# The second output gate of a sequence-encoder trunk, with 512- and 256-column products, a split moved to GpSimd, and two small moves

## The chip, the cores and the metric

The kernel runs on one NeuronCore of a Trainium2 chip. The metric is the device time of one execution in microseconds; three executions of the kernel before were timed, and one more was profiled. TensorE (PE in the rows) does the matrix products and the loads of their stationary operands, VectorE (DVE), ScalarE (ACT) and GpSimd (POOL) do the elementwise work, SyncE (SP) and ScalarE issue the DMAs used here.

## The reference, cut to what matters

Two layers work on x of 256 positions by 1024 channels, in float32. Each layer mixes tokens (an mLSTM branch beside a convolution branch), attends to 256 memory tokens and applies a gated FFN. The part touched here:

```python
h = rmsnorm(x, norm_mix[l])
p = h @ w_in[l] + b_in[l]
y_m = mlstm_branch(p[..., :o1], p[..., o1:o2], ...)
y_c = conformer_conv_branch(p[..., o2:o3], p[..., o3:o4], ...)   # conv of 31 taps -> layernorm -> silu -> @ w_pw
merged = sigmoid(p[..., o4:o5]) * y_m + sigmoid(p[..., o5:]) * y_c
x = x + merged @ w_out[l]
```

The first gate, sigmoid(p[o4:o5]), is called g1 below, the second g2.

## The kernel before, in words

**Numbers as two parts.** Every large product is computed from float32 numbers that are split into a high part (rounded to the engine's fast format) and the rest, the low part. A product is the sum of three: high by high, high by low and low by high. Activations stand channel by position: 8 channel tiles of 128 rows, each with 256 high and 256 low columns side by side. Weights come in chunks of 256 output columns, a chunk as two halves of 128; one half and its 8 channel tiles are one block of PE's work.

**Two forms of a block.** `three` (L100 to L104) runs, for each channel tile, three products of 256 columns into one accumulator of 256 columns: 24 products, each with a weight load of its own. `two` (L90 to L98) runs 8 products of 512 columns, high weights by high and low activations at once, into an accumulator of 512 columns, and then 8 products of 256 columns, low weights by high activations, into its second part: 16 products, 16 loads and as many columns in sum. The two parts of that accumulator must then be added: `joined` (L281) copies the second part to a scratch tile on ACT (L285, or L287 with a bias) and adds it to the first on DVE (L288). `proj` (L299) takes `two` with halves=True. In mix(), mdown uses `two` for chunks 0 and 1 and pw for chunks 0 to 2; g1 and g2 use `three`.

**Weights.** `weights` (L194) runs loads and splits ahead of use: a load of 1 MB a chunk by DMA (L169), then for each half the high part on ACT (L184, a cast of 1024 columns) and the low part either on DVE (L190, one subtraction of 1024 columns) or, where the table ON_POOL (L39) names the chunk, on POOL (L188, two of 512 columns). Splits run four halves ahead of the products. Five split halves and three raw chunks fit at a time.

**Accumulators.** Blocks go to three PSUM banks in turn (`acc`). A bank is free when the last reader of its block is done; for pw that is the split of the merged result (ACT L267, DVE L268).

**Order.** Each engine runs its instructions in a fixed order. The framework lays that order down when the kernel is built, from the program's order, priorities and its own model of the durations. The list `portions` holds small pieces of work (convolution taps on DVE, then the layer norm) of which a few are taken after each block (`taps`).

**Start.** The first chunk is used unsplit, in full float32 (`proj_first`, L291). emit_loads (L159) issues its first half in two pieces and its second half whole on SP's queue (L166), while ACT's queue brings x in four pieces (L211); then ACT loads its function table and computes one dummy value (L225). Chunks 1 and 2 are loaded from ACT's queue (L169) as soon as x is being scaled (L979, L273). Here x is scaled by the norm's weights alone; the row of 1/rms is multiplied into the results later. The sums of squares for it are products with a column of means (`stats`, L333), followed by an addition on DVE (L336) and a power on POOL (L338); `to_row` (L372) spreads the result over rows with four small products (L324) and a copy on ACT (L377). Where these stand among PE's products is given by hooks, (half, channel tile) of a chunk: (0, 7) and (1, 6) everywhere.

**Layer norm of the convolution.** POOL adds the four pairs of channel tiles into ysum (L495), two tiles wide, the last pair when the last tap is done. `ln_mean` (L696) multiplies both tiles of ysum by a matrix of 1/1024 on PE in full float32 (L699). Then come the differences (L703), squares (L706) and their sums.

Of the kernel before, what the change touches and what calls it, by code (L numbers as in the profile page):

```python
# [11 lines left out]
ALU = mybir.AluOpType  # L12
# [7 lines left out]
KT = D // P  # L20
# [16 lines left out]
HEADS_AT = ((0, 1), (2, 3), (), ())  # L37

ON_POOL = {"xm": (3,), "g": (0, 1, 2, 3), "a": (0, 1, 2, 3), "k": (0, 1, 2, 3), "v": (0, 1),  # L39
           "z": (0, 2, 3), "pw": (1, 3), "g1": (0, 1, 2, 3), "g2": (0, 1), "wo": (0, 1, 2),  # L40
           "uv": tuple(range(1, 11))}


# [14 lines left out]
def trunk(ctx, tc, xT, memT, pvec, wgr, w_in, ml_w_down, cv_w_pw, w_out, xa_wq, xa_wk, xa_wv, xa_wo,  # L58
# [100 lines left out]
    def emit_loads(upto):  # L159
        while st["dma"] < min(upto, len(chunks)):  # L160
            i = st["dma"]
            ap = chunks[i][1]
            raws[i] = wraw.tile([P] + list(ap.shape[1:]), F32, tag="raw", name=nm("raw"))
            if i == 0:
                for j, sl in ((0, slice(0, KT // 2)), (0, slice(KT // 2, KT)), (1, slice(0, KT))):
                    nc.sync.dma_start(raws[i][:, j, sl], ap[:, j, sl])  # L166
                halves.extend(raws[0][:, j] for j in range(2))
            else:
                (nc.scalar if i <= LATE_LOADS else nc.sync).dma_start(raws[i], ap)  # L169
            st["dma"] += 1  # L170
# [46 lines left out]
    with tc.high_priority():  # L217

        nc.vector.memset(mean1, 1.0 / D)
        early = sm([P, P])  # L220
        for _ in range(WARM):
            nc.tensor.matmul(early, mean1, mean1, start=True, stop=True)
        nc.vector.memset(zero1, 0.0)
        with tc.issue_after(loaded.ins):
            table = nc.scalar.activation(const.tile([4, 1], F32, name="early"), zero1, AF.Silu)  # L225
    make_identity(nc, ident)
    mhalf = const.tile([P, 8], F32, name="mhalf")
    nc.gpsimd.memset(mhalf, -0.5)
# [28 lines left out]
    def col(l, name, i, n=1):  # L257
        o = _COLS[name] + i
        return pvs[l][:, o:o + n]
# [39 lines left out]
    def proj(key, x2, hooks=None, halves=False, bank=None):  # L299


        done = []
        for j, w in weights(key):
            ps = (bank or acc)([P, 2, S] if halves else [P, S])
            if halves:
                last["pe"] = two(ps, [(w[:, :, k, :], x2[:, k]) for k in range(KT)], True, True)
                yield j, ps
                continue
            for k in range(KT):
                last["pe"] = three(ps, w[:, :, k, :], x2[:, k], k == 0, k == KT - 1)  # L310
                if hooks and (j, k) in hooks:
                    with tc.issue_after(last["pe"].ins):
                        hooks[j, k]()
            if hooks:
                done.append((j, ps))
            else:
                yield j, ps
        yield from done
# [97 lines left out]
    def mix(l, x):  # L416
        xc, hs = planes("xch")
        at, ready, norms = int(l == 0), [], list(range(4))
        hooks = x.hooks()
        for i in range(4):  # L420
            for j, ps in (proj_first(("xm", l, i), xf) if l + i == 0 else
                          proj(("xm", l, i), x.u, hooks if i == at else None, bank=sm if i == 1 and at else None)):
# [59 lines left out]
        def glu(i):  # L482
            sg = t2(F32, "sg")
            for j, ps in proj(("g", l, i), x2):
                last["act"] = nc.scalar.activation(sg[:, j, :], ps, AF.Sigmoid,
                                                   bias=col(l, "b_in", 24 + 2 * i + j))
                taps(TAPS["glu"])
            for j, ps in proj(("a", l, i), x2):
                c = 2 * i + j
                nc.vector.scalar_tensor_tensor(u31[:, c, CK - 1:], ps, col(l, "b_in", 16 + c), sg[:, j, :],  # L490
                                               op0=ALU.add, op1=ALU.mult)
                taps(TAPS["glu"])
            portions.append(lambda: conv31(i))
            if i > 0:
                portions.append(lambda: nc.gpsimd.tensor_tensor(  # L495
                    ysum, u31[:, 0:2, CK - 1:] if i == 1 else ysum, u31[:, 2 * i:2 * i + 2, CK - 1:], op=ALU.add))

        ysum = t2(F32, "ysum")
        glu(0)
# [195 lines left out]

        def ln_mean():  # L696
            ln["pm"] = sm([P, S])
            for n in range(2):
                nc.tensor.matmul(ln["pm"], mean1, ysum[:, n, :], start=(n == 0), stop=(n == 1))  # L699

        def ln_square(c2):
            sl = slice(2 * c2, 2 * c2 + 2)
# [12 lines left out]

        for n, o, dst in (("g1", 32, s1), ("g2", 40, s2)):
            for i in range(4):
                for j, ps in proj((n, l, i), x2):
                    c = 2 * i + j
                    nc.scalar.activation(dst[:, c, :], ps, AF.Sigmoid, bias=col(l, "b_in", o + c))  # L720
                    taps(TAPS["g"])
        while portions:
# [251 lines left out]

    x = Stream(0, "nmix")
    xf = planes("xf")[0]
    with tc.high_priority(), tc.issue_after(table.ins):
        for c in range(8):
            nc.vector.tensor_scalar(xf[:, c, :], xs[:, c, :], col(0, "nmix", c), None, op0=ALU.mult)  # L979
            x.split(c)  # L980
            if c == 3:
                emit_loads(2)
        emit_loads(3)
        nc.scalar.dma_start(pvs[0][:, KT:], pvec[0][:, KT:])
# [98 lines left out]
```

## Time and profile before

| | |
|---|---|
| median of 3 timed executions | 1071.78 us (1070.57 to 1072.33) |
| the profiled execution, its own time | 1070.13 us |
| its span, first to last instruction | 1068.4 us |
| mean granted TensorE clock | 0.998 of full speed |
| PE busy | 1057.0 us (99%), 7166 products |
| DVE, ACT, POOL busy | 853.4 us (80%), 699.2 us (65%), 438.5 us (41%) |
| share of the chain that ended last | PE 48% by the page's list, all of its lines products |

A PE product's duration in the trace contains its way through the pipeline, so products overlap: 256 columns show 0.28 us, but start 0.12 us apart. What a stage costs is read from the starts.

### The profile page before, as it was taken

The page shows a single profiled execution, that of the slowest core. Times are in us where ns is not written, and L with a number is a line of the kernel's source. Part 1 is how long each engine was busy: PE and PEld are TensorE (multiplying, and loading weights), DVE is VectorE, ACT ScalarE, POOL GpSimd, SP SyncE. Part 2 cuts the span into 40 slices and gives each one's busy share as a digit, 9 for nine tenths or more (in the row PEclk, how much of TensorE's full clock was granted, in tenths as well). Part 3 has the DMA queues.
Part 4 walks back from the last instruction along what each step waited for, and adds up shares of the span by engine and source line. Part 5 has one row for each costly group of instructions (what it writes and reads, how often), then busy time and mean ns, then how long its engine had stood idle before and what let it go on. Part 6 is the DMA issues. An engine that isn't in the chain of part 4 may idle for free. (4 is left out here: it accounts for less than half of the span.)

```text
span 1068.4 us, 18718 instructions
## 1 busy us (share of the span) xinstructions
PE 1057.0 (99%) x7166; PEld 977.8 (92%) x7166; DVE 853.4 (80%) x1731; ACT 699.2 (65%) x1152; POOL 438.5 (41%) x351
## 2 busy tenths in 40 slices
PE   8999999999999999999999999999999999999997
PEld 8999889999998988888899998999999989888886
DVE  5899898988857887786587988998788589787753
ACT  5887576466655787774477766565655658877642
POOL 2869568414041354520056784781210414535000
PEclk9999999999999999999999999999999999999999
DMA  8545436455533465555555364555465345555551
GB/s 288 186 149 163 153 122 234 159 198 197 191 129 121 153 203 200 190 197 182 191 179 190 120 198 140 197 170 194 148 222 174 119 158 173 183 197 178 178 197 39
DMA packets 46777, 185.84 MB, mean 174 GB/s; under 512 B 3168, under 2 KB 3168, under 8 KB 44128
## 3 DMA queue, kind: packets, MB, share of 16 engines
q1 hardware_dynamic: 44128, 176.70, 48.5%
q10 hardware_dynamic: 2560, 7.96, 2.2%
q8 instruction: 56, 0.92, 0.3%
q14 instruction: 33, 0.27, 0.1%
HBM read 183.60 MB, written 1.05 MB: 173 GB/s over the span
## 5 line engine op out<-in xcount | busy, mean ns | idle before, releaser
L188 POOL TENSOR_TENSOR wsp<-raw,wsp 128x512 fp32r<-128x512 f32 x312 | 406.0, 1330 | 274.6 <-ACT wsp L184 261.1
L184 ACT CAST wsp<-raw 128x1024 fp32r<-128x1024 f32 (+2 forms) x342 | 352.4, 1036 | 148.8 <-PE acc L104 60.3
L190 DVE TENSOR_TENSOR wsp<-raw,wsp 128x1024 fp32r<-128x1024 f32 (+2 forms) x186 | 233.6, 1258 | 65.5 <-ACT wsp L184 63.0
L477 DVE SCALAR_TENSOR_TENSOR cv<-u,pv,cv 128x256 f32<-128x256 f32 x464 | 193.6, 479 | 2.8 <-ACT cv L470 2.7
L102 PE MATMUL acc<-x,wsp 128*128 128x256 f32 x640 | 182.7, 286 | 0.0
L103 PE MATMUL acc<-x,wsp 128*128 128x256 f32 x640 | 182.0, 284 | 0.0
L104 PE MATMUL acc<-x,wsp 128*128 128x256 f32 x640 | 181.4, 284 | 0.0
L95 PE MATMUL acc<-x,wsp 128*128 128x512 f32 x576 | 144.2, 392 | 0.0
L103 PEld LDWEIGHTS acc<-x,wsp 128*128 128x128 f32 x640 | 122.7, 192 | 0.4 <-issue 0.2
L102 PEld LDWEIGHTS acc<-x,wsp 128*128 128x128 f32 x640 | 122.6, 192 | 0.4 <-issue 0.2
L104 PEld LDWEIGHTS acc<-x,wsp 128*128 128x128 f32 x640 | 122.7, 192 | 0.0
L95 PEld LDWEIGHTS acc<-x,wsp 128*128 128x128 f32 x576 | 103.6, 189 | 18.5
L338 POOL TENSOR_TENSOR rv<-rv,mhalf 128x2 f32<-128x2 f32 x8 | 6.5, 816 | 231.4 <-DVE rv L336 231.4
L878 DVE SCALAR_TENSOR_TENSOR fy<-u,pv,fy 128x256 f32<-128x256 f32 x176 | 84.1, 484 | 20.4 <-ACT fy L875 19.1
L102 PE MATMUL acc<-u,wsp 128*128 128x256 f32 x352 | 99.7, 286 | 0.0
L103 PE MATMUL acc<-u,wsp 128*128 128x256 f32 x352 | 99.7, 284 | 0.0
L104 PE MATMUL acc<-u,wsp 128*128 128x256 f32 x352 | 99.4, 283 | 0.0
L97 PEld LDWEIGHTS acc<-x,wsp 128*128 128x128 f32 x576 | 78.6, 190 | 5.6
L97 PE MATMUL acc<-x,wsp 128*128 128x256 f32 x576 | 80.3, 282 | 0.0
L103 PEld LDWEIGHTS acc<-u,wsp 128*128 128x128 f32 x352 | 67.5, 192 | 0.3
L104 PEld LDWEIGHTS acc<-u,wsp 128*128 128x128 f32 x352 | 67.4, 192 | 0.0
L102 PEld LDWEIGHTS acc<-u,wsp 128*128 128x128 f32 x352 | 67.1, 192 | 0.2
(302 smaller groups left out, 2143.2 us busy)
## 6 DMA issues: line engine op xcount, KB each, us to landing
raw<-in_w_in_dram SPq DMA_DIRECT2D x45, 1024.0 KB, 4.9
raw<-in_ffn_w_up_dram SPq DMA_DIRECT2D x44, 1024.0 KB, 4.8
raw<-in_w_down_last_dram SPq DMA_DIRECT2D x10, 1024.0 KB, 4.8
raw<-in_xa_wk_dram SPq DMA_DIRECT2D x8, 1024.0 KB, 4.8
raw<-in_xa_wv_dram SPq DMA_DIRECT2D x8, 1024.0 KB, 5.1
raw<-in_ml_w_down_dram SPq DMA_DIRECT2D x8, 1024.0 KB, 4.8
raw<-in_cv_w_pw_dram SPq DMA_DIRECT2D x8, 1024.0 KB, 4.9
raw<-in_w_out_dram SPq DMA_DIRECT2D x8, 1024.0 KB, 5.0
```

What stands on the lines that cost most here:

```text
L95: nc.tensor.matmul(ps, a[:, 0], b, start=first and n == 0, stop=False)
L97: mm = nc.tensor.matmul(ps[:, 1], a[:, 1], b[:, 0], start=False, stop=last and n == len(pairs) - 1)
L102: nc.tensor.matmul(ps, a[:, 0], b[:, 0], start=first, stop=False)
L103: nc.tensor.matmul(ps, a[:, 0], b[:, 1], start=False, stop=False)
L104: return nc.tensor.matmul(ps, a[:, 1], b[:, 0], start=False, stop=last)
L184: nc.scalar.copy(hi, r)
L188: nc.gpsimd.tensor_tensor(lo[:, sl], r[:, sl], hi[:, sl].bitcast(F32), op=ALU.subtract)
L190: nc.vector.tensor_tensor(lo, r, hi.bitcast(F32), op=ALU.subtract)
L338: nc.gpsimd.tensor_tensor(rv, v, mhalf[:, 0:2], op=ALU.pow)
L477: nc.vector.scalar_tensor_tensor(o, u31[:, c, k:k + S], col(l, "cdw", c * CK + k), cv[j], op0=ALU.mult, op1=ALU.add)
L878: nc.vector.scalar_tensor_tensor(y[:, j, :], u[:, j, k:k + S], col(l, "fdw", 3 * c + k), y[:, j, :], op0=ALU.mult, op1=ALU.add)
```

## The change

g2 takes `two` for all four chunks, with `joined` (at a priority raised by 100) ahead of its sigmoid; chunk 2 of g2 and chunk 2 of pw get their low parts on POOL; the second half of the first chunk is loaded from ACT's queue, behind x and behind ACT's dummy value, and the scaling of x is put behind that load; the hooks of mix() stand at (1, 1) and (1, 6) in layer 0 (chunk 1) and at (0, 7) and (1, 7) in layer 1 (chunk 0); POOL adds the two tiles of ysum into one, and ln_mean multiplies that one alone.

```diff
-           "z": (0, 2, 3), "pw": (1, 3), "g1": (0, 1, 2, 3), "g2": (0, 1), "wo": (0, 1, 2),
+           "z": (0, 2, 3), "pw": (1, 2, 3), "g1": (0, 1, 2, 3), "g2": (0, 1, 2), "wo": (0, 1, 2),
...
-                for j, sl in ((0, slice(0, KT // 2)), (0, slice(KT // 2, KT)), (1, slice(0, KT))):
-                    nc.sync.dma_start(raws[i][:, j, sl], ap[:, j, sl])
+                for sl in (slice(0, KT // 2), slice(KT // 2, KT)):
+                    nc.sync.dma_start(raws[i][:, 0, sl], ap[:, 0, sl])
...
             table = nc.scalar.activation(const.tile([4, 1], F32, name="early"), zero1, AF.Silu)
+
+        with tc.issue_after(table.ins):
+            loaded = nc.scalar.dma_start(raws[0][:, 1], chunks[0][1][:, 1])
...
-        hooks = x.hooks()
+        hooks = {(1, 1): x.stats, (1, 6): x.to_row} if at else {(0, 7): x.stats, (1, 7): x.to_row}
...
+            if i == 3:
+                portions.append(lambda: nc.gpsimd.tensor_tensor(ysum[:, 0], ysum[:, 0], ysum[:, 1], op=ALU.add))
...
-            for n in range(2):
-                nc.tensor.matmul(ln["pm"], mean1, ysum[:, n, :], start=(n == 0), stop=(n == 1))
+            nc.tensor.matmul(ln["pm"], mean1, ysum[:, 0, :], start=True, stop=True)
...
-                for j, ps in proj((n, l, i), x2):
+                for j, ps in proj((n, l, i), x2, halves=n == "g2"):
                     c = 2 * i + j
+                    if n == "g2":
+                        with tc.high_priority(offset=100):
+                            ps = joined(ps)
                     nc.scalar.activation(dst[:, c, :], ps, AF.Sigmoid, bias=col(l, "b_in", o + c))
                     taps(TAPS["g"])
...
-    with tc.high_priority(), tc.issue_after(table.ins):
+    with tc.high_priority(), tc.issue_after(loaded.ins):
         for c in range(8):
             nc.vector.tensor_scalar(xf[:, c, :], xs[:, c, :], col(0, "nmix", c), None, op0=ALU.mult)
```

## Rows read from the trace of the kernel before

**Rows 1.** The page, busy time by engine: us, share of the span, instructions.
```profile
PE 1057.0 (99%) x7166; PEld 977.8 (92%) x7166; DVE 853.4 (80%) x1731; ACT 699.2 (65%) x1152; POOL 438.5 (41%) x351
```
**Rows 2.** Timeline, layer 0, end of g2 and start of mdown: start, us, engine, line.
```profile
191.46 0.47 ACT L720 ACTIVATE xch<-acc,pv 128x256 f32<-128x256 f32 x1 [1.47 <-PE acc L104]
...
214.50 0.48 ACT L720 ACTIVATE xch<-acc,pv 128x256 f32<-128x256 f32 x1 [1.47 <-PE acc L104]
...
220.91 2.00 PE L95 MATMUL acc<-o,wsp 128*128 128x512 f32 x8
...
223.70 0.63 PE L95 MATMUL acc<-o,wsp 128*128 128x512 f32 x2
```
**Rows 3.** The stretch 197 to 221 us, busy us of each engine, PEclk, DMA share, GB/s.
```profile
197.00:221.00 24.00, 24.00 (x199) 23.89 (x198) 20.45 (x41) 12.65 (x19) 4.56 (x3) 1.00 0.40 140
```
**Rows 4.** The scratch tile of joined: minimum, median, maximum ns, first and last start.
```profile
L288 DVE TENSOR_TENSOR acc<-acc,wh x20: 417/433/433, 226.3 to 786.7; 128x256 f32<-128x256 f32 x20
L285 ACT COPY wh<-acc x8: 372/373/373, 223.9 to 757.4; 128x256 f32<-128x256 f32 x8
```
**Rows 5.** Timeline of PE around ln_mean, layer 0.
```profile
216.69 0.28 PE L104 MATMUL acc<-x,wsp 128*128 128x256 f32 x1
216.81 1.02 PE L699 MATMUL sm<-ysum,mean 128*128 128x256 f32 x4
...
217.79 0.28 PE L103 MATMUL acc<-x,wsp 128*128 128x256 f32 x1
```
**Rows 6.** POOL's additions into ysum: one line's instructions, then the last of layer 0.
```profile
L495 POOL TENSOR_TENSOR ysum<-u x2: 1288/1292/1297, 142.5 to 661.9; 128x512 f32<-128x512 f32 x2
...
212.57 3.18 POOL L495 TENSOR_TENSOR ysum<-ysum,u 128x512 f32<-128x512 f32 x1 [14.19 <-DVE u L477]
```
**Rows 7.** Timeline of PE, layer 1, the row of 1/rms.
```profile
542.60 0.28 PE L104 MATMUL acc<-u,wsp 128*128 128x256 f32 x1
543.09 0.71 PE L324 MATMUL sm<-ident,rv 128*128 128x128 f32 x4 [0.21 <-POOL rv L338]
```
**Rows 8.** Timeline of the start, all engines.
```profile
7.11 0.61 DVE L979 TENSOR_SCALAR xf<-xs,pv 128x256 f32<-128x256 f32 x2 [6.05 <-DMA xs<-in_xT_dram]
...
9.08 1.93 DVE L979 TENSOR_SCALAR xf<-xs,pv 128x256 f32<-128x256 f32 x6 [1.35 <-DMA xs<-in_xT_dram]
9.09 0.39 ACTq L169 DMA_DIRECT2D raw<-in_w_in_dram  x1
...
9.49 6.31 PE L296 MATMUL acc<-xf,raw 128*128 128x256 f32 x28 [0.84 <-DVE xf L979]
...
13.91 2.00 ACT L184 CAST wsp<-raw 128x1024 fp32r<-128x1024 f32 x2 [2.02 <-DMA raw<-in_w_in_dram]
```
**Rows 9.** Stretches of the start; the last two numbers are DMA share and GB/s.
```profile
8.00:9.00 1.00, 0.65 (x4) 0.22 (x2) 0.00 (x0) 0.00 (x0) 0.00 (x0) 1.00 0.92 356
9.00:10.00 1.00, 0.51 (x2) 0.49 (x3) 0.92 (x4) 0.92 (x3) 0.00 (x0) 1.00 0.15 57
10.00:11.00 1.00, 1.00 (x6) 0.87 (x6) 0.92 (x5) 1.00 (x3) 0.00 (x0) 1.00 0.96 139
```
**Rows 10.** Timeline of PE, layer 0, statistics and row.
```profile
19.60 1.05 PE L333 MATMUL cm<-mean,sq 128*128 128x1 f32 x8 [0.43 <-DVE sq L990]
...
22.86 0.60 PE L324 MATMUL sm<-ident,rv 128*128 128x128 f32 x4
```
**Rows 11.** Timeline of the stage pw, layer 0: PE, DVE, POOL.
```profile
264.59 0.39 PE L102 MATMUL acc<-c,wsp 128*128 128x256 f32 x1 [0.28 <-DVE g L268]
...
245.94 1.98 DVE L190 TENSOR_TENSOR wsp<-raw,wsp 128x1024 fp32r<-128x1024 f32 x1
...
257.45 1.23 DVE L190 TENSOR_TENSOR wsp<-raw,wsp 128x1024 fp32r<-128x1024 f32 x1
...
262.97 1.23 DVE L190 TENSOR_TENSOR wsp<-raw,wsp 128x1024 fp32r<-128x1024 f32 x1
...
252.06 5.13 POOL L188 TENSOR_TENSOR wsp<-raw,wsp 128x512 fp32r<-128x512 f32 x4 [0.73 <-ACT wsp L184]
```

## The prediction, made before the changed kernel was run

> **What bounds the kernel now.** I read the page's busy times first: PE is busy 99% of the span, DVE 80%, ACT 65%, POOL 41% [rows 1]. Because products overlap in the trace I then read PE's timeline by starts. From the first block at full pace to the last, PE's products follow each other almost everywhere at their own distance; what a change takes out of PE's queue comes off the time, and what it does to the other engines counts only where one of them makes PE wait. So I looked for the places where PE waits: the start, where it waits for x and then for the sum of squares [rows 8, 10]; the row of 1/rms in layer 1 [rows 7]; and one accumulator in the stage pw [rows 11]. The change touches all three, and PE's own work in two more.
>
> **Part 1, g2 as two products.** A block of `three` takes 2.88 us: the sigmoids behind nine such blocks start at 191.46 to 214.50, eight distances in 23.04 us [rows 2]. A block of `two` takes 2.79 us, from 220.91 to 223.70 [rows 2]: as many columns, eight weight loads fewer. That is 0.087 us a block by the finer starts, call it 0.09; 8 blocks in each of 2 layers give 16 x 0.09 = 1.4 us. A rule of the Trainium skill (TensorE: Matmul & The Clock Gate, section Back-to-back issue gap) puts a product at its columns divided by 2.4 GHz plus 2.5 ns, which would leave only 2.5 ns for each pair made into one, an estimate of 16 x 8 x 2.5 ns = 0.3 us, and 2.4 us instead of 3.5 for the whole sum. I take the rows, since both forms stand in them at the full clock.
>
> What it adds lies on the other engines: per block a copy on ACT of 0.37 us and an addition on DVE of 0.43 us [rows 4]. In the stretch of g2 ACT has 24 - 12.7 us free and DVE 24 - 20.5 us [rows 3]; 8 x 0.43 = 3.5 us would fill DVE, but the two low parts of chunk 2 (2 x 1.23 us, [rows 11]) leave it. Who waits behind these? The bank of a block is held through copy, addition and sigmoid. With a cast of 1.0 us [rows 8] in front of each ACT step and a subtraction of 1.2 us in front of DVE's, that is 1.0 + 0.4 + 1.2 + 0.4 + 1.0 + 0.5 = 4.5 us, and PE comes back to the bank after two blocks, 5.6 us. I cost it at nothing; if that cover were gone, it would be up to 1 us in a layer.
>
> **Part 2, ln_mean.** Its four records (two products, each in two passes) put 217.79 - 216.69 = 1.10 us between products that would stand 0.24 apart without them: 0.86 us, 0.43 for one product [rows 5]. One goes, in two layers: 0.86 us. In its place POOL adds 256 columns. POOL's own rows show 1.29 us for 512 [rows 6], so 0.65 us, up to half of 3.18 = 1.6 where it is held up as the last one was [rows 6]. ysum is complete at 212.57 + 3.18 = 215.75, and PE takes it up at 216.81: 1.06 us to spare [rows 5, 6]. After the change PE arrives 0.6 us sooner (six and a half g2 blocks) and ysum 0.65 to 1.6 later, so if PE's order keeps its place it may wait 0.2 to 1.2 us in a layer. The order is laid down anew, though, with the addition in it, so I take no wait and keep 1.1 us a layer for the bounds; nor do I take a gain there.
>
> **Part 3, the row in layer 1.** PE stands from 542.72 (0.12 after 542.60) to 543.09 for the power on POOL [rows 7]. Three products more, 0.36 us, go in front of the row: -0.36 us, and the row comes when it came before.
>
> **Part 4, the first loads.** x lands late: DVE scales two tiles at 7.11, then waits, and the rest starts at 9.08; PE starts its steady run at 9.49 [rows 8]. The second half of chunk 0, 0.5 MB, travels among x on the other queue. At 356 GB/s [rows 9] it takes 1.4 us; put behind x it lets x finish about 1.3 us sooner, and PE's run starts near 8.2. That is not yet the gain, for what follows hangs on chunk 1: its DMA is issued at 9.09, when x is there, and its cast waits until 13.91 [rows 8]. The queue is nearly empty from 9 to 10 and slow until 11 (57 and 139 GB/s, [rows 9]). Now the half chunk fills that hole: x done near 7.8, chunk 1 issued then, the half chunk done near 10.3, and chunk 1's 1 MB at some 380 GB/s behind it near 13.0, 0.9 us sooner than now. Casts, squares and their sums follow in order on ACT and DVE, and PE's place for the row is bound by that chain (19.60 to 22.86 is statistics, addition, power and nothing else [rows 10]), so 0.9 us it is. Bounds: +0.5 us, if the half chunk is late for PE's second block (needed near 10.4, there near 10.3), and -2.0 us, if both PE's waits at the start and the one at 19.60 go.
>
> **Part 5, the hooks of layer 0.** The statistics move six products later: PE waited at least 0.43 us at that place [rows 10]. But the row stays at (1, 6), and between the two are then 15 products, 1.8 us, for a chain of 3.26 us less the statistics' own 0.9. What is saved at the first place is waited for at the second: 0.
>
> **Part 6, pw's chunk 2 on POOL.** At 264.59 PE has waited for a bank, 0.28 us by the row [rows 11] and 0.44 by the starts, and layer 1 does the same. The bank is freed by DVE's split, which stands behind a subtraction of 1.23 us at 262.97 [rows 11]; that one belongs to the next weight (out) and stays. DVE loses the subtraction at 245.94 [rows 11] and the one after it, but it had idle time between its steps again before the next, at 257.45 [rows 11]. So I take 0. Bounds: -0.9 us (both waits go, by a new order) and +1.5 us: POOL, now with twelve instructions instead of eight, works until about 259 rather than 252.06 + 5.13 = 257.19 and meets the subtraction at 257.45 [rows 11]. What such a meeting costs is shown at 245.94, where the subtraction took 1.98 instead of 1.23 us beside POOL: 0.75 us, in two layers.
>
> **The sum.** -1.4 - 0.86 - 0.36 - 0.9 + 0 + 0 = -3.5 us. The profiled execution took 1070.13 us with its span of 1068.4; it becomes 1066.6. That execution lies 1.65 us under the median of the three shown, so against the median I say 1071.78 - 3.5 = 1068.3 us.
>
> **Rivals.** (a) *The pw wait goes too, or the start gives more.* A new order puts DVE's split ahead of the subtraction: 0.9 us more, 1067.4; with a start at its bound, 1066.3. For it: DVE has 2.5 us less to do there; against: the wait stands at an instruction that stays. (b) *The gains of PE are waited away:* PE meets ln_mean before POOL's second addition in both layers, -3.5 + 2 x 1.1 = -1.3, or the start gives nothing besides; 1070.5 to 1071.4. For it: the last addition took 3.18 us instead of 1.29 [rows 6]; against: the order has room for POOL's step. (c) *POOL holds DVE, slower:* each subtraction on DVE that meets one of POOL's waits for its end, up to 1.3 us. If POOL's four added instructions push its work so far that the three subtractions from 257.45 to 262.97 all meet one, DVE's chain is 3.9 us late in each layer, PE waits that at the banks, and 7.8 - 3.5 = +4.3 gives 1076.1. It decides from 5.6 us of such waits in all on. For it: the two durations above; against: PE's blocks let POOL finish by about 259, and only one subtraction lies before that. The Trainium skill (SBUF — State Buffer, section Who interferes with whom) says that a DVE instruction with two SBUF inputs and a GpSimd instruction that reads SBUF exclude each other for a whole instruction, whichever began first; 1.98 against 1.23 us and 3.18 against 1.29 agree with that. (d) *Fewer loads give nothing but the issue,* as the rule under part 1 has it: -2.4, 1069.4. The rows speak against it at every block of either form. (e) *The change does not do what it says at the start:* x is slow for another reason than the half chunk, -2.6, 1069.2; at 8 to 9 us the queues run at 356 GB/s, which speaks for shared bandwidth.
>
> **The numbers.** A measurement of this kernel can tell about 0.2%, 2.1 us, from no change. Forecast 0.42, (a) 0.18, (d) 0.02, (e) 0.10: all faster by more than that, 0.72. (b) 0.23: within it. (c) 0.05: slower. The range leaves out (c) and the far ends of (a) and (b): 1066.0 to 1070.9. It takes in the bounds of parts 4 and 6.
>
> **What would show it.** In the changed profile: g2 blocks of 2.79 us and 128 fewer products in g2; two records instead of four at ln_mean and no wait in front of them; no wait in front of layer 1's row; x scaled without a break from about 7.7 and chunk 1 cast near 13.0; the wait of 0.44 us at pw unchanged. The forecast is wrong if PE waits for POOL at ln_mean, if a wait in pw grows past 1 us, if a bank is waited for in g2 or mdown, or if chunk 1 is cast no sooner than before.

## The result, and the profile after

The changed kernel is slower: 1082.16 us (median of 4 runs, 1081.69 to 1083.14) against 1071.82 us before (1070.57 to 1072.33), a ratio of 1.0104 with a 95% interval of 1.0091 to 1.0116. The forecast was 1068.3 us, faster. The profiled execution took 1083.14 us, its span is 1081.4 us against 1068.4. In the changed file the lines stand three to seven further down: the norm's products L699 are L703, the row L324 is L327, the power L338 is L341, the additions of `joined` L288 are L291 and its copies L285 are L288, the taps L477 are L480, ysum's additions L495 are L498, and L501 is the new one.

First the page's busy times of the changed kernel, beside [rows 1].

```profile
PE 1060.1 (98%) x7034; PEld 974.4 (90%) x7034; DVE 849.9 (79%) x1739; ACT 704.6 (65%) x1168; POOL 458.0 (42%) x369
```

132 products are gone, as planned (128 in g2, 4 at ln_mean), and yet PE is busy longer. Stretches at a lower clock are what lengthens products; they will be seen below. The list of PE's waits of the changed kernel (engine, line, what it waited for: us in total, times, longest) names the places where it stands still (the three longest in total of eight lines; the others lie at the start or are 0.5 us or less):

```profile
PE sm L703 <- POOL ysum L501: 4.8, 2, 2.6
PE sm L327 <- POOL rv L341: 4.4, 1, 4.4
PE acc L102 <- DVE g L271: 1.5, 2, 1.2
```

**The start.** Timeline of the changed kernel, DVE, ACT, POOL and PE between 6 and 28 us (answers to [rows 8, 10]):

```profile
6.55 2.46 DVE L986 TENSOR_SCALAR xf<-xs,pv 128x256 f32<-128x256 f32 x8 [5.49 <-DMA xs<-in_xT_dram]
...
12.84 1.99 ACT L184 CAST wsp<-raw 128x1024 fp32r<-128x1024 f32 x2 [2.69 <-DMA raw<-in_w_in_dram]
...
20.66 0.15 DVE L339 TENSOR_SCALAR rv<-cm 128x2 f32<-128x2 f32 x1
...
21.55 1.99 ACT L184 CAST wsp<-raw 128x1024 fp32r<-128x1024 f32 x2 [2.74 <-DMA raw<-in_w_in_dram]
...
22.68 2.48 POOL L188 TENSOR_TENSOR wsp<-raw,wsp 128x512 fp32r<-128x512 f32 x2 [19.88 <-ACT wsp L184]
25.12 0.71 POOL L341 TENSOR_TENSOR rv<-rv,mhalf 128x2 f32<-128x2 f32 x1
...
21.19 0.28 PE L104 MATMUL sm<-u,wsp 128*128 128x256 f32 x1
25.89 1.22 PE L327 MATMUL sm<-ident,rv 128*128 128x128 f32 x4 [4.42 <-POOL rv L341]
```

x is scaled without a break from 6.55, and chunk 1 is cast at 12.84 instead of 13.91: the early part is about 1.1 us ahead. At 20.81 the sum of squares is ready for POOL's power. But in POOL's order the power now stands behind two splits of the last chunk of xm, and these wait for a cast at 21.55, which waits for its DMA. The power begins at 25.12, and PE, whose last product before the row starts at 21.19, stands for it until 25.89: 4.57 us by the starts, that is the distance between two starts less the usual one (0.12 us after 256 columns, 0.23 after 512). DVE's step (L339) comes late too: the statistics' products end at 18.52 + 1.05 = 19.57, but two subtractions stand in front of it until 20.66. In the kernel before, the order was the other way round:

```profile
20.94 1.62 POOL L338 TENSOR_TENSOR rv<-rv,mhalf 128x2 f32<-128x2 f32 x1 [18.14 <-DVE rv L336]
22.89 5.07 POOL L188 TENSOR_TENSOR wsp<-raw,wsp 128x512 fp32r<-128x512 f32 x4 [0.34 <-ACT wsp L184]
```

And the wait has an echo. Stretches of the changed kernel, busy us of PE, PEld, DVE, ACT, POOL, then PEclk, DMA share, GB/s:

```profile
24.00:25.00 1.00, 0.00 (x0) 0.00 (x0) 0.00 (x0) 0.00 (x0) 1.00 (x1) 0.72 0.95 389
25.00:27.00 2.00, 1.11 (x5) 1.11 (x6) 0.00 (x0) 0.00 (x0) 2.00 (x3) 0.50 0.12 43
27.00:31.00 4.00, 4.00 (x21) 4.00 (x21) 2.69 (x7) 3.60 (x8) 3.40 (x4) 0.50 0.40 108
```

While PE stands, the granted clock falls to 0.50, the level of 1.2 GHz, and stays there for some 5.4 us after PE has resumed. Products of 256 columns then start 0.21 us apart instead of 0.12:

```profile
28.83 0.41 PE L102 MATMUL acc<-u,wsp 128*128 128x256 f32 x1
29.04 0.41 PE L103 MATMUL acc<-u,wsp 128*128 128x256 f32 x1
```

About 2.5 of these 5.4 us are lost, by comparison with the same products in the first experiment below, which run at full clock. At PE's first products with the memory tokens the changed kernel is 5.48 us behind the kernel before, 88.59 against 83.11:

```profile
88.59 0.50 PE L336 MATMUL sm<-mean,mem 128*128 128x1 f32 x4
```

**The norm of the convolution.** PE, DVE and POOL around ln_mean of the changed kernel, layer 0 (answers to [rows 2, 5, 6]):

```profile
218.92 2.00 PE L95 MATMUL acc<-x,wsp 128*128 128x512 f32 x8
...
221.71 1.09 PE L95 MATMUL acc<-x,wsp 128*128 128x512 f32 x4
225.07 0.70 PE L703 MATMUL sm<-ysum,mean 128*128 128x256 f32 x2 [2.26 <-POOL ysum L501]
...
205.56 0.43 DVE L291 TENSOR_TENSOR acc<-acc,wh 128x256 f32<-128x256 f32 x1 [1.97 <-ACT wh L288]
205.90 2.05 DVE L480 SCALAR_TENSOR_TENSOR cv<-u,pv,cv 128x256 f32<-128x256 f32 x5
208.35 0.43 DVE L291 TENSOR_TENSOR acc<-acc,wh 128x256 f32<-128x256 f32 x1 [0.40 <-ACT wh L288]
...
220.31 0.87 DVE L480 SCALAR_TENSOR_TENSOR u<-u,pv,cv 128x256 f32<-128x256 f32 x2
...
221.26 2.10 POOL L498 TENSOR_TENSOR ysum<-ysum,u 128x512 f32<-128x512 f32 x1 [12.15 <-DVE u L480]
223.43 1.58 POOL L501 TENSOR_TENSOR ysum<-ysum 128x256 f32<-128x256 f32 x1
```

A block takes 221.71 - 218.92 = 2.79 us, as forecast. But DVE has lost its lead. POOL takes up the last pair, with the last tap done, at 221.26; PE would have come to ln_mean at 225.07 - 2.43 = 222.64, only 1.4 us later. In the kernel before it was 212.57 for 216.81 [rows 5, 6], 4.2 us, and DVE then had nothing to do but to wait for the mean:

```profile
217.88 0.69 DVE L703 TENSOR_TENSOR u<-u,sm 128x512 f32<-128x512 f32 x1 [3.18 <-PE sm L699]
```

In the changed kernel, at 205.56, DVE stands 1.97 us in front of the first addition of `joined`, which needs PE's block and ACT's copy, and then 0.4 us in front of three of the following. POOL needs 2.10 + 1.58 us, and PE stands 2.43 us by the starts (2.73 in layer 1). In this execution a stretch at half clock follows both waits; it begins as PE resumes or shortly after, not while PE stands (at 225.07 PE resumes, and from 225 to 226 the mean is still 0.91):

```profile
225.00:226.00 1.00, 0.93 (x4) 0.83 (x5) 0.19 (x1) 0.00 (x0) 0.01 (x1) 0.91 1.00 414
226.00:229.00 3.00, 3.00 (x13) 2.71 (x12) 1.69 (x3) 0.63 (x1) 0.00 (x0) 0.50 0.19 76
...
748.00:751.00 3.00, 2.99 (x7) 2.42 (x8) 1.75 (x3) 1.25 (x3) 0.00 (x0) 0.51 0.54 220
```

**pw.** Layer 0 of the changed kernel, PE's wait for a bank, DVE and POOL in front of it (answers to [rows 11]):

```profile
274.38 0.39 PE L102 MATMUL acc<-c,wsp 128*128 128x256 f32 x1 [1.21 <-DVE g L271]
...
265.91 2.87 DVE L190 TENSOR_TENSOR wsp<-raw,wsp 128x1024 fp32r<-128x1024 f32 x1
...
257.61 10.08 POOL L188 TENSOR_TENSOR wsp<-raw,wsp 128x512 fp32r<-128x512 f32 x8
```

DVE's subtraction meets the last of POOL's splits, which follow each other without a break, and takes 2.87 us instead of 1.23. The 1.64 us more are longer than one of these splits (10.08 / 8 = 1.26 us): it was held past one and through the next. PE's wait grows from 0.44 to 1.37 us by the starts. In layer 1 it stays at 0.44.

**The row of layer 1** comes without a wait, and across it the changed kernel gains the forecast 0.36 us:

```profile
552.75 0.28 PE L104 MATMUL acc<-u,wsp 128*128 128x256 f32 x1
552.88 0.49 PE L327 MATMUL sm<-ident,rv 128*128 128x128 f32 x2
```

### The profile page after: what moved, and what is told of

Read it like the earlier page. It is cut to its first block, busy times and chain, and to the rows that moved or that the text cites. A ratio compares the mean times of both kernels' runs of the same rounds, so it can differ in the third digit from the quotient of the medians.

```text
span 1081.4 us, 18513 instructions
## 1 busy us (share of the span) xinstructions
PE 1060.1 (98%) x7034; PEld 974.4 (90%) x7034; DVE 849.9 (79%) x1739; ACT 704.6 (65%) x1168; POOL 458.0 (42%) x369
## 3 DMA queue, kind: packets, MB, share of 16 engines
HBM read 183.60 MB, written 1.05 MB: 171 GB/s over the span
## 4 chain that ended last, share of the span: by engine, by line
PE 93%; DVE 2%; POOL 1%; DMA 1%; ACT 1%; issue 1%; POOLq 0%; ACTq 0%; DVEq 0%
PE acc L95 26%; PE acc L102 14%; PE acc L103 14%; PE acc L104 14%; PE acc L97 14%; PE sm L102 2%; PE sm L103 2%; PE sm L104 2%; DVE wsp L190 1%; PE sm L536 1%; DMA raw<-in_w_in_dram 1%; PE sm L525 1%; PE acc L299 1%; PE sm L515 1%; DVE cv L480 0%
## 5 line engine op out<-in xcount | busy, mean ns | idle before, releaser
L188 POOL TENSOR_TENSOR wsp<-raw,wsp 128x512 fp32r<-128x512 f32 x328 | 423.7, 1324 | 292.4 <-ACT wsp L184 269.3
L190 DVE TENSOR_TENSOR wsp<-raw,wsp 128x1024 fp32r<-128x1024 f32 (+1 forms) x178 | 224.0, 1261 | 62.6 <-ACT wsp L184 60.1
L480 DVE SCALAR_TENSOR_TENSOR cv<-u,pv,cv 128x256 f32<-128x256 f32 x464 | 193.8, 479 | 2.8 <-ACT cv L473 2.7
L95 PE MATMUL acc<-x,wsp 128*128 128x512 f32 x704 | 178.9, 396 | 0.0
L95 PEld LDWEIGHTS acc<-x,wsp 128*128 128x128 f32 x704 | 128.0, 191 | 23.1
L102 PE MATMUL acc<-x,wsp 128*128 128x256 f32 x512 | 146.1, 286 | 0.0
L103 PE MATMUL acc<-x,wsp 128*128 128x256 f32 x512 | 145.7, 285 | 0.0
L104 PE MATMUL acc<-x,wsp 128*128 128x256 f32 x512 | 145.2, 284 | 0.0
L97 PEld LDWEIGHTS acc<-x,wsp 128*128 128x128 f32 x704 | 96.9, 192 | 7.0
L97 PE MATMUL acc<-x,wsp 128*128 128x256 f32 x704 | 98.9, 284 | 0.0
L103 PEld LDWEIGHTS acc<-x,wsp 128*128 128x128 f32 x512 | 98.1, 192 | 0.3 <-issue 0.2
L102 PEld LDWEIGHTS acc<-x,wsp 128*128 128x128 f32 x512 | 98.0, 192 | 0.3 <-issue 0.2
L104 PEld LDWEIGHTS acc<-x,wsp 128*128 128x128 f32 x512 | 98.1, 192 | 0.0
L341 POOL TENSOR_TENSOR rv<-rv,mhalf 128x2 f32<-128x2 f32 x8 | 6.5, 816 | 211.4 <-DVE rv L339 211.4
L103 PEld LDWEIGHTS acc<-u,wsp 128*128 128x128 f32 x352 | 68.3, 194 | 0.3
L104 PEld LDWEIGHTS acc<-u,wsp 128*128 128x128 f32 x352 | 68.2, 194 | 0.0
L102 PEld LDWEIGHTS acc<-u,wsp 128*128 128x128 f32 x352 | 67.9, 194 | 0.2
```

The lines of the kernel that those rows point to most:

```text
L95: nc.tensor.matmul(ps, a[:, 0], b, start=first and n == 0, stop=False)
L97: mm = nc.tensor.matmul(ps[:, 1], a[:, 1], b[:, 0], start=False, stop=last and n == len(pairs) - 1)
L102: nc.tensor.matmul(ps, a[:, 0], b[:, 0], start=first, stop=False)
L103: nc.tensor.matmul(ps, a[:, 0], b[:, 1], start=False, stop=False)
L104: return nc.tensor.matmul(ps, a[:, 1], b[:, 0], start=False, stop=last)
L188: nc.gpsimd.tensor_tensor(lo[:, sl], r[:, sl], hi[:, sl].bitcast(F32), op=ALU.subtract)
```

## The experiments

The theories are numbered alike in all expectations: 1, the hook at (1, 1) puts the power behind POOL's splits; 2, the additions of `joined` stand in DVE's fixed order and tie DVE to PE's pace, and POOL's new addition within ysum adds to that (2a: because of the raised priority); 3, pw's chunk 2 on POOL holds DVE up. Their rivals stand in the expectations. Ratios are against the kernel before, timed beside the run, with their 95% intervals.

**1. Undo the hook of layer 0 alone, in the changed kernel.**

```diff
-        hooks = {(1, 1): x.stats, (1, 6): x.to_row} if at else ...
+        hooks = {(0, 7): x.stats, (1, 6): x.to_row} if at else ...
```

> The changed kernel with one part undone: in layer 0 the statistics are back at (0, 7). Theory 1 (order on POOL): moved to (1, 1), the power stands behind two weight splits in POOL's order, and these wait for chunk 3's load; PE stands 4.57 us at the row and then runs at the half clock. Undone, the power comes first again, the row's products start near 21.6 us (25.89 in the changed kernel, 22.86 in the one before), no half clock follows, and the whole comes down by 6.9 us, to about 1075.3. Rival (early loads): the late row comes from the load put on ACT's queue; then the wait stays, and the time stays near 1082.

Measured: 1075.70 us, ratio 1.0041 (1.0029 to 1.0053). Where one hook stands is worth 0.63%, 6.7 us (with an interval of about 1.8 us to either side). POOL and PE of this kernel:

```profile
19.51 1.62 POOL L341 TENSOR_TENSOR rv<-rv,mhalf 128x2 f32<-128x2 f32 x1 [16.71 <-DVE rv L339]
21.77 2.55 POOL L188 TENSOR_TENSOR wsp<-raw,wsp 128x512 fp32r<-128x512 f32 x2 [0.64 <-ACT wsp L184]
...
21.45 0.49 PE L327 MATMUL sm<-ident,rv 128*128 128x128 f32 x3
...
81.92 0.50 PE L336 MATMUL sm<-mean,mem 128*128 128x1 f32 x4
```

The power goes first again, the row comes at 21.45 without a wait, 1.41 us sooner than before the change, and the clock keeps its full level from 20 to 31 us. At the first products with the memory tokens this kernel is 88.59 - 81.92 = 6.67 us ahead of the changed one, so the whole price lies in front of them. The two waits at ln_mean are unchanged (2.43 and 2.73 us), but in this profile only the one of layer 1 has a stretch at half clock behind it; in layer 0 the clock stays up:

```profile
220.00:223.00 3.00, 2.96 (x17) 2.63 (x18) 1.88 (x3) 0.91 (x3) 0.00 (x0) 1.00 0.55 225
```

That prices such a stretch: from ln_mean to the first product of pw this kernel takes 26.44 us (220.04 to 246.48) and the changed kernel 27.96 (225.07 to 253.03), 1.5 us more after the same wait. The wait in pw is back at 0.49 us here, though pw's chunk 2 is still on POOL: DVE's subtraction came between POOL's last two splits and took 1.63 us, and POOL's last split took 2.29.

```profile
259.36 1.63 DVE L190 TENSOR_TENSOR wsp<-raw,wsp 128x1024 fp32r<-128x1024 f32 x1
```

**2. Undo the new addition: ln_mean multiplies both tiles again, in the changed kernel.**

```diff
-            if i == 3:
-                portions.append(lambda: nc.gpsimd.tensor_tensor(ysum[:, 0], ysum[:, 0], ysum[:, 1], op=ALU.add))
...
-            nc.tensor.matmul(ln["pm"], mean1, ysum[:, 0, :], start=True, stop=True)
+            for n in range(2):
+                nc.tensor.matmul(ln["pm"], mean1, ysum[:, n, :], start=(n == 0), stop=(n == 1))
```

> The changed kernel without POOL's second addition: ln_mean multiplies both tiles of ysum again. Theory 2 (DVE stands still): ysum itself is late, because DVE stands idle in front of the new additions of g2 until PE's block and ACT's copy are done; then PE still waits at ln_mean, about 1.2 us in layer 0 (2.43 now) and 1.3 in layer 1 (2.73 now), but perhaps without the half clock behind it: about 1077 to 1080. Rival (the addition alone): without it no wait is left in either layer and the time is about 1074.4.

Measured: 1076.31 us, 1.0039 (1.0027 to 1.0052). The waits at ln_mean are 1.23 and 1.30 us, 1.2 and 1.4 us less, and the clock stays up after them. The row of the start still waits 4.2 us, and the wait in pw is back at 0.48 us.

```profile
222.88 1.13 PE L702 MATMUL sm<-ysum,mean 128*128 128x256 f32 x4 [1.06 <-POOL ysum L498]
```

So the addition has only part of the waits, 2.6 us. The rest of its price is the clock: two stretches of 3.4 us at half speed, some 1.5 us lost in each.

**3. g2 as three products again, in the changed kernel.**

```diff
-                for j, ps in proj((n, l, i), x2, halves=n == "g2"):
+                for j, ps in proj((n, l, i), x2):
...
-                    if n == "g2":
-                        with tc.high_priority(offset=100):
-                            ps = joined(ps)
```

> The changed kernel with g2 back in the form of 24 products of 256 columns, all other parts kept. Theory 2 (DVE stands still in front of the additions of joined): DVE has no idle time in g2, the last tap ends some 3 us earlier against PE, and the waits at ln_mean shrink to under 0.6 us without a half clock: g2's own products cost 1.4 us more, the sum is about 1077. Rival (POOL's second addition, or its split of chunk 2): the waits of 2.4 and 2.7 us stay, and the time goes up by 1.4 us to about 1083.5.

Measured: 1074.72 us, 1.0028 (1.0016 to 1.0040). With the new addition still there, PE waits at ln_mean in neither layer. DVE and POOL of this kernel in layer 0:

```profile
204.60 9.10 DVE L480 SCALAR_TENSOR_TENSOR cv<-u,pv,cv 128x256 f32<-128x256 f32 x23
...
216.09 3.25 POOL L498 TENSOR_TENSOR ysum<-ysum,u 128x512 f32<-128x512 f32 x1 [6.09 <-DVE u L480]
219.41 0.74 POOL L501 TENSOR_TENSOR ysum<-ysum 128x256 f32<-128x256 f32 x1
```

DVE runs 23 taps in a row where the changed kernel has five or six between two additions. It is the additions of `joined` that take its lead. The wait in pw is now 1.37 us in both layers, with a subtraction of 2.63 us on DVE in front of the first. The time is 2 us lower than theory 2 gave.

**4. Only g2 as two products, in the kernel before (and its chunk 2 on POOL).**

```diff
-           ... "g2": (0, 1), ...
+           ... "g2": (0, 1, 2), ...
...
-                for j, ps in proj((n, l, i), x2):
+                for j, ps in proj((n, l, i), x2, halves=n == "g2"):
...
+                    if n == "g2":
+                        with tc.high_priority(offset=100):
+                            ps = joined(ps)
```

> The kernel before with g2 alone changed: products of 512 and 256 columns, joined at raised priority, chunk 2 split on POOL. Theory 2: g2's blocks give 1.4 us back, DVE stands idle about 3 us in front of the additions, and PE waits about 1.2 us at ln_mean in each layer: about 1072.5, no gain. Rival (the forecast's working): DVE keeps up, no wait, 1070.4.

Measured: 1072.26 us, 1.0010 (1.0001 to 1.0020). PE's own gain of 1.4 us is more than taken back by waits of 1.23 and 1.30 us at ln_mean, with no stretch at half clock behind them. The new form and the move of chunk 2 to POOL were not tried apart, but in this kernel POOL stands idle for 12.15 us in layer 0 and 6.07 in layer 1 until the last tap is done, so its splits didn't hold ysum up. What DVE waited for in this kernel from 195 to 226 us:

```profile
DVE acc L288 <- ACT wh L285: 4.1, 5, 2.0
```

**5. Only the first loads and the hook of layer 1, in the kernel before.**

```diff
-                for j, sl in ((0, slice(0, KT // 2)), (0, slice(KT // 2, KT)), (1, slice(0, KT))):
-                    nc.sync.dma_start(raws[i][:, j, sl], ap[:, j, sl])
+                for sl in (slice(0, KT // 2), slice(KT // 2, KT)):
+                    nc.sync.dma_start(raws[i][:, 0, sl], ap[:, 0, sl])
...
+        with tc.issue_after(table.ins):
+            loaded = nc.scalar.dma_start(raws[0][:, 1], chunks[0][1][:, 1])
...
-        hooks = x.hooks()
+        hooks = {(0, 7): x.stats, (1, 6): x.to_row} if at else {(0, 7): x.stats, (1, 7): x.to_row}
...
-    with tc.high_priority(), tc.issue_after(table.ins):
+    with tc.high_priority(), tc.issue_after(loaded.ins):
```

> The kernel before with two parts of the change: the second half of chunk 0 on ACT's queue behind x, and the row of layer 1 at (1, 7); layer 0's hooks stay. Theory: both are gains by themselves, 1.2 us at the row of layer 0 (near 21.6 us) and 0.36 us in layer 1: about 1069.6, and nothing lost later. Rival: what the start gives is waited away in a later stage of layer 0 (PE waited 1.6 us at the transposes of z in the run with the hook back); then the time is within 0.5 us of the kernel before.

Measured: 1069.19 us, 0.9986 (0.9976 to 0.9995). The row of layer 0 comes at 21.65, 1.21 us sooner, and layer 1's row gives the 0.36.

**6. As the fourth experiment, at the ordinary priority.**

```diff
-                        with tc.high_priority(offset=100):
-                            ps = joined(ps)
+                        ps = joined(ps)
```

> The kernel before with g2 in products of 512 and 256 columns and chunk 2 on POOL, but joined at its own place in the program's order, without raised priority. Theory 2a (the raised priority puts the additions ahead of taps that could run): DVE's idle time in g2 falls from about 3 us to under 1, no wait at ln_mean, about 1.4 us faster than before, 1069.8. Rival 2b (DVE meets the additions too early whatever their priority): idle time and the waits of 1.23 and 1.30 us stay, as in the run with g2 alone: about 1072.

Measured: 1073.75 us, 1.0030 (1.0021 to 1.0040), no better. In layer 0 DVE keeps its lead and ln_mean doesn't wait, but now the addition stands behind the norm's sums (L708), and PE waits for the bank in front of mdown, 2.23 us by the starts, with a stretch at half clock behind it. In layer 1 DVE stands 3.3 us before an addition all the same, and PE 1.30 us at ln_mean. Timeline of this kernel, layer 0:

```profile
224.08 2.45 PE L95 MATMUL acc<-o,wsp 128*128 128x512 f32 x6 [2.07 <-ACT xch L722]
...
222.32 0.42 DVE L288 TENSOR_TENSOR acc<-acc,wh 128x256 f32<-128x256 f32 x1
```

So variant 2a is half wrong: the priority chooses which of two things is late, the taps or the banks.

**7. Only pw's chunk 2 on POOL, in the kernel before.**

```diff
-           ... "pw": (1, 3), ...
+           ... "pw": (1, 2, 3), ...
```

> The kernel before with chunk 2 of pw split on POOL and nothing else. Theory 3 (POOL and DVE exclude each other): the first subtraction of the next weight on DVE meets POOL's later work and takes 2.6 to 2.9 us instead of 1.23, and PE's wait for a bank grows from 0.44 to 1.37 us: up to 1.9 us slower in two layers, about 1073. Rival (no meeting): waits of 0.44 us stay, no difference. Second rival (DVE is relieved): the waits go, 0.9 us faster.

Measured: 1071.19 us, 0.9998 (0.9987 to 1.0009). The meeting is there but milder than in the changed kernel, 1.83 us for DVE's subtraction and a wait of 0.67 us instead of 0.44:

```profile
261.56 1.83 DVE L190 TENSOR_TENSOR wsp<-raw,wsp 128x1024 fp32r<-128x1024 f32 x1
```

Theory 3 was too large for the edit alone. Nor do the other edits settle it: with the same split on POOL the wait is 0.5 us in the first and second experiments and 1.37 in the third. What differs there is how many of POOL's splits DVE's subtraction has to let pass.

**8. The fifth and the sixth together.** The diffs are theirs.

> Early loads, layer 1's row at (1, 7), g2 in products of 512 and 256 columns with chunk 2 on POOL and joined without raised priority; layer 0's hooks, ln_mean and pw as before. Theory (the parts add up): the gains of the two runs above together, 1.6 + 1.4 = 3.0 us: about 1068.2. Rival 2b: g2's gain is waited away, about 1070 to 1071.

Measured: 1072.97 us, 1.0018 (1.0009 to 1.0028): waits of 2.23 us at mdown in layer 0 and 1.30 at ln_mean in layer 1 as in the sixth, less the gain of the fifth. Neither the theory's 1068.2 nor the rival's 1070 to 1071 came; the two ratios taken one after the other do give 1.0016.

**9. The changed kernel with the last chunk of xm split on DVE, so that POOL has nothing in front of the power.**

```diff
-ON_POOL = {"xm": (3,), ...
+ON_POOL = {"xm": (), ...
```

> The changed kernel, hooks at (1, 1) and (1, 6) kept, but chunk 3 of xm is split on DVE instead of POOL, so POOL has no split to do before the power. Theory 1 (the power is late only because two splits stand ahead of it in POOL's order): the row of layer 0 starts near 21.8 us instead of 25.89, no half clock follows, and the time falls by about 6.5 us to 1075.6. Rival (the later place itself makes it late, by the shorter stretch between the hooks): the row stays near 25 us and the time near 1081.

Measured: 1085.66 us, 1.0138 (1.0124 to 1.0153), slower still, which no theory had expected. At the place in question the theory holds, though: the power goes as soon as its input is there, and the row comes at 21.16, after a wait of 0.35 us by the starts (DVE's two subtractions still stand in front of its step here), with no half clock behind it. At the first products with the memory tokens this kernel is 88.59 - 83.06 = 5.53 us ahead of the changed one:

```profile
20.39 0.71 POOL L341 TENSOR_TENSOR rv<-rv,mhalf 128x2 f32<-128x2 f32 x1 [17.59 <-DVE rv L339]
...
21.16 0.60 PE L327 MATMUL sm<-ident,rv 128*128 128x128 f32 x3 [0.19 <-POOL rv L341]
...
83.06 0.50 PE L336 MATMUL sm<-mean,mem 128*128 128x1 f32 x4
```

In its own place theory 1's gain is there. What follows is another kernel: four subtractions more on DVE (182 for 178) and another order. PE's list of waits has new or longer entries in other stages, among them these:

```profile
PE sm L103 <- DVE wsp L190: 1.8, 1, 1.8
PE sm L327 <- POOL rv L341: 1.2, 2, 1.0
```

The time of the whole run therefore says nothing on theory 1; its rows do. What each of the new waits costs was not taken apart.

**10. The fifth with POOL's new addition, g2 as before.** To the fifth is added what the second took out.

> Early loads, layer 1's row at (1, 7), and POOL's second addition with ln_mean on one tile; g2 stays at 24 products a block. Theory (the addition costs nothing where DVE keeps its lead in g2): no wait at ln_mean, 0.43 us a layer on top of the run with loads and row alone: 2.5 us faster than the kernel before. Rival (the addition is late by itself): a wait of 0.5 to 1 us in each layer takes it back, and the gain is about 1.6 us or less.

Measured: 1069.02 us, 0.9976 (0.9965 to 0.9988). Where DVE keeps its lead the addition is free: its trace shows no wait at ln_mean. Against the fifth experiment the two intervals don't tell 0.9 us apart. ysum's instructions of this kernel (shortest, median, longest ns):

```profile
L501 POOL TENSOR_TENSOR ysum<-ysum x2: 737/740/742, 216.0 to 733.8; 128x256 f32<-128x256 f32 x2
```

**11. As the fourth, with ln_mean late:** behind the 512-column products of g2's last block, and the rest of the norm behind g2.

```diff
-            nc.tensor.matmul(ps, a[:, 0], b, start=first and n == 0, stop=False)
+            mid["pe"] = nc.tensor.matmul(ps, a[:, 0], b, start=first and n == 0, stop=False)
...
-            for n in range(2):
-                nc.tensor.matmul(ln["pm"], mean1, ysum[:, n, :], start=(n == 0), stop=(n == 1))
+            with tc.high_priority(offset=60), tc.issue_after(mid["pe"].ins):
+                for n in range(2):
+                    nc.tensor.matmul(ln["pm"], mean1, ysum[:, n, :], start=(n == 0), stop=(n == 1))
...
-        portions += [ln_mean] + [lambda c2=c2: ln_square(c2) for c2 in range(4)] + [ln_stats]
+        norm_of_conv = [ln_mean] + [lambda c2=c2: ln_square(c2) for c2 in range(4)] + [ln_stats]
...
+        portions += norm_of_conv
```

> The kernel before with g2 in products of 512 and 256 columns (joined at raised priority, chunk 2 on POOL) and one more edit: ln_mean is placed behind the 512-column products of g2's last block, and what follows it in the norm comes behind g2. Theory 2 (the waits of 1.23 and 1.30 us are a place that is too early, not work that PE needs): no wait at ln_mean, g2's 1.4 us come through. Rival (the norm's chain has no slack): PE waits later, at the norm's row behind mdown's chunk 1 or at the start of pw, by 1 us or more a layer, and the gain is gone.

Measured: 1070.23 us, 0.9995 (0.9986 to 1.0004). The waits at ln_mean are gone in both layers, nothing waits for the norm later, and the kernel is no slower than before; the time doesn't resolve a gain of 1.4 us.

**12. The eleventh with the fifth.**

> The run before this one with the early loads and layer 1's row at (1, 7). Theory: the gains add up to 1.2 + 0.36 + 1.4 = 3.0 us less than the kernel before. Rival: the norm's late chain takes g2's part back, and 1.5 us are left.

Measured: 1067.83 us, 0.9973 (0.9963 to 0.9983), 2.9 us faster than the kernel before, as the theory said (3.0); the rival's 1.5 lies outside the interval. It is faster than both kernels, but not told apart from the tenth experiment (0.9976), which leaves g2 as it was. PE around ln_mean in layer 0:

```profile
217.34 2.00 PE L95 MATMUL acc<-x,wsp 128*128 128x512 f32 x8
219.18 1.02 PE L703 MATMUL sm<-ysum,mean 128*128 128x256 f32 x4
```

Its profiled execution has a wait of 2.3 us near 167 us, at transposes. That wait varies between none and 2.4 us from one profile to the next, where nothing near it was changed; a single profile's total is uncertain by as much.

## Why the prediction was wrong

**Right.** The block of 2.79 us (part 1), the row of layer 1 (part 3), and the first loads (part 4): the cast of chunk 1 was forecast near 13.0 and came at 12.84, and with part 3 alone the loads gave 0.14%, 1.5 us, against a forecast of 0.36 + 0.9. The steps on the way were less well placed: x is scaled from 6.55 instead of about 7.7, and the cast came where forecast all the same. The rule of the Trainium skill that I weighed in part 1 (TensorE: Matmul & The Clock Gate, section Back-to-back issue gap) would leave a pair of products only 2.5 ns; the 0.09 us saved in a block of eight pairs are 11 ns a pair. Here the measurement decides, and rival (d) falls.

**Part 5, the hooks of layer 0, is the first step that failed.** It counted products between the two hooks and the length of the chain. Neither was wrong, but the chain's middle step is on POOL, and I never asked what stands in front of it in POOL's order. The later hook put it behind two splits which wait for a DMA. Instead of 0 the price was 4.57 us of waiting, less 0.48 us saved at the statistics, and 2.5 us of lower clock, 6.6 us; the first experiment gives back 6.7. DVE's step stood behind two subtractions as well; the ninth experiment, which clears POOL's order alone, puts that at 0.35 us.

**Part 1's cover is the second.** "I cost it at nothing" looked at how busy DVE and ACT are and how long a bank is held. The 3.5 us of DVE's free time [rows 3] were no reserve in its queue: 3.2 of them lay behind the last tap, as a wait for the mean. They were the lead that made ln_mean free. Queue order turns an addition that needs PE's block into a meeting point, so an engine that was ahead falls back to PE's pace. The price by the fourth experiment is 2.5 us of waits against a gain of 1.4. No edit of priority alone removed it; placing the consumer, ln_mean, later did.

**Part 2** took no wait because the order is laid down anew, with its own bound of 1.1 us a layer. The waits were 2.43 and 2.73 us, of which 1.2 and 1.4 go with the addition. POOL's step was 1.58 us, at the upper end that I had given, while DVE was splitting beside it; in the tenth experiment it was 0.74. So two signs that the prediction names against itself came: PE waits for POOL at ln_mean, and a wait in pw is past 1 us.

**Part 6** bounded a meeting by 0.75 us, from 1.98 against 1.23; one of 1.6 us came (2.87). The rule of the Trainium skill that I named (SBUF — State Buffer, section Who interferes with whom) agrees with a longer duration. But my bound of one meeting, and the 1.3 us for the end of one split in rival (c), are too small: the subtraction let the rest of one split and a whole second one pass. It cost PE 0.93 us, in layer 0 only, and hardly anything in the first two experiments. Rival (c), the one on the slower side, had the right sign and the wrong place: POOL did decide, at the start and by its additions, and not through the subtractions in pw.

**The clock** was missing from all bounds. In the changed kernel's profile the three waits of 2.4 to 4.6 us each came with a stretch at 1.2 GHz; the waits of 1.2 and 1.3 us in the second and fourth experiments had none. Such a stretch isn't certain: the same wait of 2.43 us had none in the first experiment, and over the four executions of the changed kernel the mean granted clock lay between 0.991 and 0.995. I had no row of the kernel before with such a stretch in the middle of the work: PE didn't stand so long there.

The account closes roughly: +6.7 for the hook (first), +1.1 for g2 with its waits (fourth), -1.5 for loads and row of layer 1 (fifth), -0.9 + 2.6 of waits + 3.0 of clock = +4.7 for the addition, and +0.9 for pw make +11.9, against 11.1 by the ratio (9.8 to 12.4). The clock terms come from single profiles. The second experiment gives 7.0 us, about 1.9 to either side, where the addition alone has 4.7: in its profile the wait in pw is 0.9 us shorter too, and the lower clock at the start lasts 3.4 us instead of 6.8.

## What to carry to other kernels

A product form that saves PE a little but adds a step on another engine has to be costed at that engine's place in the order, not by its free time: whoever was ahead must now wait for PE, and what depends on its lead comes late. When a chain moves, read the queue of every engine that it passes, for what stands in front of it and what that waits for. Where PE may come to stand for long, bound the lower clock behind the wait as well.

## What the runs showed of the hardware

With PE's waits of 2.43, 2.73 and 4.57 us in the changed kernel the granted clock was at its lower level for 3.4, 3.4 and 6.8 us. At the start it fell while PE stood, some 3 us after its last product; at ln_mean it fell at about 225.8 and 748.1 us, as PE resumed (748.01) or 0.7 us later (225.07). In these stretches 256 columns start 0.21 us apart instead of 0.12, and one of 3.4 us costs 1.5 us. The length of the wait doesn't settle whether one follows: behind 2.43 us there was one in the changed kernel and none in the first experiment, behind 2.23 us there was one (sixth experiment), and behind the 2.30 us in the last there was none.

An addition of 256 columns on POOL took 0.74 us where no subtraction of DVE was under way when it began (tenth experiment), and 1.58 us beside one; 512 columns took 1.29 us in [rows 6]. A subtraction on DVE that met POOL's splits of 1.3 us, which follow each other without a break, took 2.87 us instead of 1.23 when two of them went first (changed kernel), and 1.63 when it came between the last two (first experiment).
